# Seven-product projections of q, k and v, and the Fourier projection as a stage of its own

## The chip, the cores and the metric

The kernel runs on one core of a Trainium2 chip. The metric is the device time of one execution in microseconds. TensorE (PE) multiplies, VectorE (DVE), ScalarE (ACT) and GpSimd (POOL) work on tiles, SyncE (SP) issues DMAs, and DMA queues move data between HBM and the on-chip memory. Products accumulate in PSUM banks of 128 rows by 512 columns of fp32.

## The reference

One encoder block over 2048 tokens and 16 meta tokens put ahead of them, of width 1024:

```python
h += W_out [ RMSNorm_a(GQA attention group) ++ RMSNorm_f(Fourier group) ]  # from one W_in on RMSNorm(h)
h += W_down relu(W_up RMSNorm(h))^2
```

`W_in` has 1536 columns: 512 for q (4 heads of 128), 256 for k and 256 for v (2 heads each), and 512 for u. q and k are RMS-normed per head and rotated by an axial rope, and attention is softmax(q k^T / sqrt(128)) v over all 2064 tokens. u goes through `fft2(u, axes=(token, channel)).real` in four groups of 128 channels, and each group through a 128 by 128 matrix. Both groups are normed and go through `W_out`, the sum is the residual for a feed-forward layer of 4096 hidden units, and the 2048 real tokens leave through a last RMSNorm. All is fp32.

## The kernel before

**Arithmetic.** Each fp32 operand of a product is split in a high part (a cast on ACT, L70, or L73 with a scale per row) and a low part (source minus high on DVE, L71 or L74). `mm3` (L77) multiplies them with three matmuls, L80 to L82: high by high, high by low, low by high. `NG`=4 is the number of Fourier groups, `KT`=8 that of 128-row pieces of the width.

**Projections.** The tokens go in 8 pairs of 128. `prep(j)` (L274) norms a pair, transposes it on TensorE (L291) and splits it into `hth` and `htl`. `proj_qkv(j)` (L365) makes `pq` and `pkv` of both token tiles, each as 8 pieces by 3 matmuls of 512 columns. `proj_u(j)` (L331) makes u with the channels as rows: 4 groups by 8 pieces by 3 matmuls of 256 columns (272 in the last pair, which carries the meta tokens along). u stands in `UA`; from pair 4 on it is at once added to and subtracted from its mirror image, the sum in `EV`, the difference in `UA`. `post(j, a, ..)` (L389) works on a finished tile: squares on ACT (L408), the rest by DVE (L190, L414 to L422), transposes and splits, and stores to `q_d`, `k_d`, `v_d`, `v_n`. The weights are loaded (`wraw`) and split (`wh`, `wl`) at the start, row piece by row piece.

**Order of the work.** A generator per piece of side work is advanced between groups of matmuls (`side`), and a scheduler of the language then places each engine's instructions in the order it takes for best; the engines carry them out in that order. In the last pair, `proj_u` runs ahead of `proj_qkv`, and beside the latter run the folds (`fold`, `fold_even`, L506 to L517): each adds and subtracts halves of `EV` and `UA`, for the four groups, on DVE with a copy on ACT.

**Behind the projections.** `fourier()` (L658) makes four transforms: products `pa` with the channel matrices (L570), their splits `ahi` (ACT) and `alo` (DVE, L576), and products `py` with token tables (`thi`, `tlo`). `out_f` (L909) multiplies the result by its part of `W_out` (`pof`). Beside both runs attention, in steps counted from 0; each unit makes scores `s`, running maxima `M`, exponentials `S`, sums `acc` and products `o`. `mix(gen, n, a0, a1, skip)` advances a generator of n pieces and attention from step a0 to a1 together:

```python
    mix(with_weights(four, 9), 19, 0, FLEAD, SKIP - 1)
    mix(itertools.islice(of, 34 - HELD), 34 - HELD, FLEAD, need[0])
    mix(of, HELD, need[0], need[0] + LEAD)
```

`FLEAD` is 30 and `need[0]` is 84, so the transforms have 30 attention steps beside them and `out_f` 54. The later stages (attention's output product, `up`, `down`) are the same in both kernels; some of them use the scheme of seven products that the change brings to the projections.

## Time and profile before

| what | value |
|---|---|
| runs of the kernel | 2291.73, 2293.10, 2293.55 us (median 2293.1) |
| span of the profiled execution | 2291.4 us |
| TensorE busy | 2278.1 us, 99% |
| DVE busy | 1718.7 us, 75% |
| ACT busy | 1280.6 us, 56% |
| GpSimd busy | 184.0 us, 8% |
| granted TensorE clock | 0.9 or more of full speed in each of 40 slices |
| moved by DMA | 307.23 MB, mean 134 GB/s |

The profiled span is the time from the first to the last instruction of one execution; the runs are timed apart from it, and their median lies 1.7 us above the span. Busy time counts work alone, not the waits. In the windows, a row has a stretch of the span, then busy us and instruction count of each engine in it, the granted clock, the mean busy share of the DMA queues and their rate. In a timeline row stand the start, the length, the engine, the line, and the tiles (output, arrow, inputs).

### The profile page before, as it was taken

The numbers are of one execution on the slowest core, as the hardware profiler recorded it, in microseconds if no ns is written. First come the engines' busy times: TensorE is split into PE (matmuls) and PEld (weight loads), VectorE is DVE, ScalarE is ACT, GpSimd is POOL, SyncE is SP. The second block draws the span as 40 slices with busy tenths as digits, with TensorE's granted clock in tenths as the row PEclk, the third lists the DMA queues.
The fourth block names the chain that finished last, engine by engine and source line by source line (L and its number), as shares of the span: only waits on it lengthen the run. The fifth ranks groups of instructions, "written<-read, shape, count | busy, mean of one in ns | idle before, by whom it ended". The sixth has DMA issues, their size and how long they took to land.

```text
span 2291.4 us, 30005 instructions
## 1 busy us (share of the span) xinstructions
PE 2278.1 (99%) x10846; PEld 1883.0 (82%) x10846; DVE 1718.7 (75%) x2448; ACT 1280.6 (56%) x2303; POOL 184.0 (8%) x235
## 2 busy tenths in 40 slices
PE   9999999999999999999999999999999999999998
PEld 7888988777888888888888888888888888888887
DVE  6435588999986877986887877885875656697796
ACT  6443356566665655665765775664665545543344
POOL 2212120222000000000000100000000000200000
PEclk9999999999999999999999999999999999999999
DMA  6343252543533222333342453224454444865442
GB/s 213 100 119 102 78 169 79 190 137 120 166 117 108 96 87 79 114 114 106 97 157 87 157 175 104 92 82 170 140 177 158 152 152 156 303 193 165 129 138 83
DMA packets 178069, 307.23 MB, mean 134 GB/s; under 512 B 14960, under 2 KB 63728, under 8 KB 177536
## 3 DMA queue, kind: packets, MB, share of 16 engines
q1 hardware_dynamic: 159136, 262.89, 34.9%
q0 software_dynamic: 18640, 42.16, 6.2%
q8 instruction: 85, 1.39, 0.3%
q14 instruction: 64, 0.52, 0.1%
q10 hardware_dynamic: 144, 0.26, 0.0%
HBM read 225.27 MB, written 79.99 MB: 133 GB/s over the span
## 4 chain that ended last, share of the span: by engine, by line
PE 94%; DVE 3%; DMA 1%; ACT 1%; issue 1%; POOL 0%; SPq 0%; POOLq 0%; DVEq 0%; ACTq 0%
PE pdn L80 5%; PE pdn L82 5%; PE pdn L81 5%; PE pup L80 5%; PE pup L82 5%; PE pup L81 5%; PE s L80 3%; PE s L82 3%; PE s L81 3%; PE ux L80 2%; PE ux L81 2%; PE ux L82 2%; PE dx L80 2%; PE dx L82 2%; PE dx L81 2%; PE o L81 2%
## 5 line engine op out<-in xcount | busy, mean ns | idle before, releaser
L80 PE MATMUL pdn<-wh_dn,ah 128*128 128x512 f32 x512 | 201.5, 394 | 0.2 <-ACT r L1154 0.2
L80 PE MATMUL pup<-mTh,wh_up 128*128 128x512 f32 x512 | 201.5, 394 | 0.0
L81 PE MATMUL pup<-mTl,wh_up 128*128 128x512 f32 x512 | 200.7, 392 | 0.0
L82 PE MATMUL pup<-mTh,wl_up 128*128 128x512 f32 x512 | 200.4, 391 | 0.0
L81 PE MATMUL pdn<-wl_dn,ah 128*128 128x512 f32 x512 | 199.9, 390 | 0.0
L82 PE MATMUL pdn<-wh_dn,al 128*128 128x512 f32 x512 | 198.7, 391 | 0.0
L773 ACT COPY S<-s 128x512 f32<-128x512 f32 x256 | 148.4, 584 | 55.6 <-PE s L82 48.5
L70 ACT CAST wh_up<-wr_up 128x512 fp32r<-128x512 f32 x128 | 79.4, 620 | 164.3 <-PE pup L81 76.5
L832 DVE TENSOR_TENSOR S<-S,mb 128x1024 f32<-128x1024 f32 x128 | 154.8, 1218 | 8.4 <-ACT mb L803 8.2
L71 DVE TENSOR_TENSOR pl<-S,ph 128x512 fp32r<-128x512 f32 x196 | 132.3, 696 | 11.0 <-ACT ph L70 10.7
L833 ACT ACTIVATE S<-S 128x1024 f32<-128x1024 f32 x114 | 120.7, 1060 | 34.7 <-DVE S L832 34.1
L70 ACT CAST wh_dn<-wr_dn 128x512 fp32r<-128x512 f32 x128 | 79.1, 620 | 107.9 <-PE pdn L82 52.6
L71 DVE TENSOR_TENSOR wl_up<-wr_up,wh_up 128x512 fp32r<-128x512 f32 x128 | 87.6, 687 | 68.1 <-ACT wh_up L70 63.3
L839 DVE TENSOR_TENSOR acc<-acc,S 128x1024 f32<-128x1024 f32 x110 | 134.1, 1219 | 1.3 <-ACT S L833 1.1
L71 DVE TENSOR_TENSOR wl_dn<-wr_dn,wh_dn 128x512 fp32r<-128x512 f32 x128 | 87.2, 687 | 60.2 <-ACT wh_dn L70 51.8
L70 ACT CAST ph<-S 128x512 fp32r<-128x512 f32 x196 | 118.7, 620 | 15.9 <-PE o L82 12.5
L70 ACT CAST ah<-a 128x1024 fp32r<-128x1024 f32 x56 | 58.5, 1048 | 118.2 <-issue 60.8
L779 DVE TENSOR_TENSOR M<-M,S 128x1024 f32<-128x1024 f32 x96 | 118.0, 1229 | 6.7 <-ACT S L773 6.0
L80 PEld LDWEIGHTS pdn<-wh_dn,ah 128*128 128x128 f32 x512 | 96.1, 188 | 23.5 <-ACT r L1154 3.6
L80 PE MATMUL s<-q,kt 128*128 128x512 f32 (+1 forms) x272 | 113.0, 415 | 0.1
L82 PEld LDWEIGHTS pdn<-wh_dn,al 128*128 128x128 f32 x512 | 96.2, 188 | 19.9
L82 PEld LDWEIGHTS pup<-mTh,wl_up 128*128 128x128 f32 x512 | 96.2, 188 | 19.4
(345 smaller groups left out, 6413.0 us busy)
## 6 DMA issues: line engine op xcount, KB each, us to landing
wr_up<-in_w_up_dram SPq DMA_DIRECT2D x128, 256.0 KB, 2.8
wr_dn<-in_w_down_dram SPq DMA_DIRECT2D x128, 256.0 KB, 2.6
a<-s_d SPq DMA_DIRECT2D x42, 512.0 KB, 3.6
R<-in_w_up_dram SPq DMA_DIRECT2D x16, 1024.0 KB, 5.2
s_d<-s SPq DMA_DIRECT2D x64, 256.0 KB, 2.2
d<-in_w_down_dram SPq DMA_DIRECT2D x26, 512.0 KB, 5.0
s_d<-c SPq DMA_DIRECT2D x48, 256.0 KB, 2.4
x<-in_x_dram SPq DMA_DIRECT2D x16, 512.0 KB, 4.9
```

What stands on the lines that cost most here:

```text
L70: self.high = nc.scalar.copy(hi, src)
L71: self.low = nc.vector.tensor_tensor(lo, src, f32v(hi), op=ALU.subtract)
L80: nc.tensor.matmul(out, a[0], b[0], start=first, stop=False, skip_group_check=chain)
L81: nc.tensor.matmul(out, a[0], b[1], start=False, stop=False, skip_group_check=chain)
L82: nc.tensor.matmul(out, a[1], b[0], start=False, stop=last, skip_group_check=chain)
L773: nc.scalar.copy(S[:, i % 2], ps)
L779: nc.vector.tensor_tensor(M, M, S, op=ALU.max)
L832: nc.vector.tensor_tensor(S, S, mb, op=ALU.subtract)
L833: nc.scalar.activation(p, S, AF.Exp, scale=ISQ)
L839: nc.vector.tensor_tensor(acc, acc, p, op=ALU.add)
```

## The change

**Seven products.** For a token pair, the product of the 2 by 2 blocks (two token tiles by two halves of the width) with the 2 by 2 blocks of weights (two halves of the width by the columns of q and of k, v) is made from seven block products instead of eight. Each takes a form of the tokens (a block, or a sum or difference of blocks) and a form of the weights. `prep` makes the seven token forms from four groups of transposes; `form` splits each and stores it to HBM (`f_d`, 512 KB each). `w_forms` makes the forms of weights 3 to 7 at the start; forms 1 and 2 are plain blocks. `project` runs the products in the order 1, 2, 6, 5, 7, 3, 4, 84 matmuls of 512 columns per pair, and DVE adds partial results (`c`).

**u as a stage.** `proj_u` is gone. When the last pair is projected, the memory of the weight forms is released, and `u_forms` makes those of u over it. `u_stage` loads the stored token forms again (`hg`, 1 MB each, three buffers) and makes u for 1024 tokens at a time with products of 512 columns, 336 matmuls; `u_meta` adds 80 narrow matmuls for the meta tokens. Attention starts in this stage: 56 steps run beside it. The folds stand behind the stage, then the transforms with steps 56 to 64, and `out_f` with steps 64 to 84.

```diff
-FLEAD = 30
-SKIP = 5
+ULEAD = 56
+FLEAD = 64
+U_FIRST = 4
+HF_BUFS = 8
+W_BUFS = 16
+C_BUFS = 6
+HG_BUFS = 3
+ORDER = "1265734"
...
+    def form(j, name, src):
+        t = tp.tile([P, 2, 4, P], R32, name=f"hf{name}_{j}", tag="hf", bufs=HF_BUFS)
+        split(t[:, 0], t[:, 1], src.rearrange("p (k n) -> p k n", k=4))
+        nc.sync.dma_start(f_d[name, j // 4][:, :, j % 4], f32v(t.rearrange("p l k n -> p l (k n)")))
+        F[j, name] = t
...
+        ps = {}
+        for a in range(2):
+            for h in range(2):
+                yield
+                p = ps[a, h] = tbank(f"pt_{j}_{a}_{h}")
+                for i in range(4):
+                    k = 4 * h + i
+                    nc.tensor.transpose(p[:, i * P:(i + 1) * P], xs[j, a][:, k * P:(k + 1) * P], ident)
+                if a == 0:
+                    form(j, "12"[h], p)
+                elif h == 0:
+                    a21 = row(f"a21_{j}")
+                    nc.scalar.copy(a21, p)
+        s1, s2, s4 = (row(f"s{i}_{j}") for i in (1, 2, 4))
+        nc.vector.tensor_tensor(s1, ps[1, 1], a21, op=ALU.add)
+        nc.vector.tensor_tensor(s2, ps[0, 0], s1, op=ALU.subtract)
+        form(j, "6", s2)
+        form(j, "5", s1)
+        nc.vector.tensor_tensor(a21, a21, ps[0, 0], op=ALU.subtract)
+        form(j, "7", a21)
+        yield
+        nc.vector.tensor_tensor(s4, ps[0, 1], s2, op=ALU.add)
+        form(j, "3", s4)
+        form(j, "4", ps[1, 1])
...
+    def w_forms(k, raws, put):
+        b11, b12, b21, b22 = raws
+        g0, g1 = c_mix(k), c_mix(k + 4)
+        nc.gpsimd.tensor_tensor(b11, b12, b11, op=ALU.subtract)
+        nc.scalar.activation(b22, b22, AF.Copy, scale=g1)
+        split(*put("5"), b11, g0)
+        nc.vector.scalar_tensor_tensor(b11, b11, g0, b22, op0=ALU.mult, op1=ALU.subtract)
+        yield
+        split(*put("6"), b11)
+        yield
+        nc.vector.scalar_tensor_tensor(b12, b12, g0, b22, op0=ALU.mult, op1=ALU.subtract)
+        split(*put("7"), b12)
+        yield
+        split(*put("3"), b22)
+        yield
+        nc.vector.scalar_tensor_tensor(b21, b21, g1, b11, op0=ALU.mult, op1=ALU.add)
+        split(*put("4"), b21)
...
+    for k in range(KT):
+        load_w(k, 512)
+    for k in (4, 0, 5, 1, 6, 2, 7, 3):
         load_w(k, 0)
     drain(prep(0))
     load_x(1)
     for k in range(KT):
+        split(*W["12"[k // 4]][k % 4], raws[k, 512], c_mix(k))
+    drain(*[w_forms(k, [raws[i] for i in ((k, 512), (k, 0), (k + 4, 512), (k + 4, 0))],
+                    lambda n, k=k: W[n][k]) for k in range(4)])
+    ws.release()
...
+    def project(j, nxt):
+        X, Y, c = None, None, {}
+        for name in ORDER:
+            if name == "1":
+                X = bank(f"px_{j}")
+            elif name in "25":
+                Y = bank(f"py{name}_{j}")
+            o = Y if name in "253" else X
+            t = F.pop((j, name))
+            for k in range(4):
+                mm3(nc, o, (t[:, 0, k], t[:, 1, k]), W[name][k], name in "125" and k == 0, k == 3, True)
+            if name in "165":
+                c[name] = cp.tile([P, 512], F32, name=f"c{name}_{j}", tag="c", bufs=C_BUFS)
+                nc.scalar.copy(c[name], o)
+            elif name == "4":
+                pend.append(post(j, 1, c["5"], X))
+            else:
+                of = c[{"2": "1", "7": "5", "3": "6"}[name]]
+                nc.vector.tensor_tensor(of, of, o, op=ALU.add)
+                if name == "3":
+                    pend.append(post(j, 0, c["6"], c["1"]))
+            side(nxt)
...
+    for j in range(LAST + 1):
...
+        project(j, nxt)
+        drain(nxt)
+    spread_m()
+    pm = bank("pkv_m")
+    for k in range(KT):
+        t = MT_["m"][k // 4]
+        mm3(nc, pm[:MR], (t[:, 0, k % 4], t[:, 1, k % 4]), W["12"[k // 4]][k % 4], k == 0, k == KT - 1)
+    pend.append(post("m", 0, None, pm))
...
+    wq.release()
...
+    chan_dft()
...
+    def u_forms():
+        for k in range(4):
+            r = tp.tile([P, D], F32, name=f"wur_{k}", tag="x", bufs=3).rearrange("p (l n) -> p l n", l=2)
+            for i in range(2):
+                nc.sync.dma_start(r[:, i], w_in[(k + 4 * i) * P:(k + 4 * i + 1) * P, 1024:1536])
+            put = lambda n: (WU[n][:, 0, k], WU[n][:, 1, k])
+            b = [r[:, 0, :256], r[:, 0, 256:], r[:, 1, :256], r[:, 1, 256:]]
+            split(*put("1"), b[0], c_mix(k))
+            split(*put("2"), b[2], c_mix(k + 4))
+            drain(w_forms(k, b, put))
...
+    def u_stage():
+        for b in range(2):
+            X, Y = {}, {}
+            def place(t, G, s):
+                if b == 0:
+                    return t[:, G, META:META + 1024].rearrange("p (c s n) -> p c s n", s=2, n=P)[:, :, s]
+                return t[:, G, 1:1025].rearrange("p (c s n) -> p c s n", s=2, n=P)[:, :, 1 - s]
+            for name in ORDER:
+                h = []
+                for e in range(2):
+                    h.append(hg.tile([P, 4, 4, P], R32, name=f"hg{name}_{b}_{e}", tag="hg", bufs=HG_BUFS))
+                    nc.sync.dma_start(f32v(h[e].rearrange("p c k n -> p c (k n)")), f_d[name, b][:, e])
+                for g in range(2):
+                    if name == "1":
+                        X[g] = bank(f"ux_{b}_{g}")
+                    elif name in "25":
+                        Y[g] = bank(f"uy{name}_{b}_{g}")
+                out = lambda g: (Y if name in "253" else X)[g]
+                for e in range(2):
+                    for g in range(2):
+                        for k in range(4):
+                            for l in range(2 - e):
+                                nc.tensor.matmul(out(g).rearrange("p (c n) -> p c n", n=P),
+                                                 WU[name][:, l, k, g * P:(g + 1) * P], h[e][:, :, k],
+                                                 start=name in "125" and e + k + l == 0, stop=e == 1 and k == 3,
+                                                 skip_group_check=True)
+                        if e == 1:
+                            G, s = {"1": (g, 0), "6": (2 + g, 0), "5": (2 + g, 1), "4": (g, 1),
+                                    "2": (g, 0), "7": (2 + g, 1), "3": (2 + g, 0)}[name]
+                            y = out(g).rearrange("p (c n) -> p c n", n=P)
+                            d = place(UA, G, s)
+                            if b:
+                                y = y[:, ::-1, ::-1]
+                                v = place(EV, G, s)
+                                nc.vector.tensor_tensor(v, v if name in "273" else d, y, op=ALU.add)
+                                nc.vector.tensor_tensor(d, d, y, op=ALU.subtract)
+                            elif name in "273":
+                                nc.vector.tensor_tensor(d, d, y, op=ALU.add)
+                            else:
+                                nc.scalar.copy(d, y)
+                    yield
...
+    u_forms()
+    us = u_stage()
+    for _ in range(U_FIRST):
+        side()
+        next(us)
+    u_meta()
+    drain(*pend)
...
+    mix(us, 28 - U_FIRST, 0, ULEAD)
+    wu.release()
+    hg.release()
+    ft = Lines(tc.alloc_tile_pool(name="ft", bufs=1, reuse_waits="tile"), small)
+    for src in (EV, UA):
+        for g in range(NG):
+            fold(src, g)
+        for g in range(0, NG, 2):
+            fold_even(src, g)
+    load_tables(0)
+    fp = Lines(tc.alloc_tile_pool(name="fp", bufs=1, reuse_waits="tile"), small)
+    four = fourier()
...
-    mix(with_weights(four, 9), 19, 0, FLEAD, SKIP - 1)
+    mix(with_weights(four, 10), 20, ULEAD, FLEAD)
```

The next rows show DVE at the start, before: `wl1024` are lows of the weights of q, k and v, in the order of the row pieces, and `htl` lows of the first token pair.

```order
L74 SCALAR_TENSOR_TENSOR wl1024_0_213<-wraw0_0_141,cols_94,wh1024_0_212 128x512
L71 TENSOR_TENSOR htl_0_0_182<-pt_0_0_176,hth_0_0_181 128x512
L74 SCALAR_TENSOR_TENSOR wl1024_0_213<-wraw512_0_143,cols_94,wh1024_0_212 128x512
L71 TENSOR_TENSOR htl_0_1_191<-pt_0_1_185,hth_0_1_190 128x512
L74 SCALAR_TENSOR_TENSOR wl1024_1_219<-wraw0_1_145,cols_94,wh1024_1_218 128x512
L71 TENSOR_TENSOR htl_0_2_200<-pt_0_2_194,hth_0_2_199 128x512
L71 TENSOR_TENSOR htl_0_3_209<-pt_0_3_203,hth_0_3_208 128x512
L74 SCALAR_TENSOR_TENSOR wl1024_1_219<-wraw512_1_147,cols_94,wh1024_1_218 128x512
L74 SCALAR_TENSOR_TENSOR wl1024_2_225<-wraw0_2_149,cols_94,wh1024_2_224 128x512
```

After, at the same engine, the last rows ahead of the first addition of a partial result (`c1`): `wl4_0` to `wl4_3` are lows of the weight form 4, which the seventh product of the first pair reads, and L343 makes that form.

```order
L343 SCALAR_TENSOR_TENSOR wraw512_5_213<-wraw512_5_213,cols_83,wraw512_1_205 128x512
L343 SCALAR_TENSOR_TENSOR wraw512_6_215<-wraw512_6_215,cols_83,wraw512_2_207 128x512
L77 TENSOR_TENSOR wl4_0_193<-wraw512_4_211,wh4_0_192 128x512
L77 TENSOR_TENSOR wl4_1_195<-wraw512_5_213,wh4_1_194 128x512
L77 TENSOR_TENSOR wl4_2_197<-wraw512_6_215,wh4_2_196 128x512
L343 SCALAR_TENSOR_TENSOR wraw512_7_217<-wraw512_7_217,cols_83,wraw512_3_209 128x512
L232 TENSOR_TENSOR sm_1_0_417<-ss_1_0_412 128x1
L232 TENSOR_TENSOR sm_1_1_429<-ss_1_1_424 128x1
L191 TENSOR_SCALAR ms_x_419<-sm_1_0_417 128x1
L191 TENSOR_SCALAR ms_x_431<-sm_1_1_429 128x1
L77 TENSOR_TENSOR wl4_3_199<-wraw512_7_217,wh4_3_198 128x512
L481 TENSOR_TENSOR c1_0_410<-c1_0_410,py2_0_436 128x512
```

The weights' lows came one by one with the products that read them; now there are sums of blocks ahead of them, and the last low stands behind all other forms.

DVE at the folds, before: the last folds of `UA`, the copies of the remainder and the splits of tables stand ahead of the normalization of the pair's tiles (`qn`), which waits for the products of q and of k, v.

```order
L516 TENSOR_TENSOR folde2_3114<-UA_69 128x514
L536 COPY rem0_3122<-EV_70 128x4x2
L536 COPY rem0_3122<-EV_70 128x4x3
L517 TENSOR_TENSOR UA_69<-UA_69 128x2x257
L536 COPY rem0_3122<-EV_70 128x4x2
L536 COPY rem0_3122<-EV_70 128x4x3
L536 COPY rem0_3122<-EV_70 128x4x2
L536 COPY rem0_3122<-EV_70 128x4x3
L551 TENSOR_TENSOR tlo0_1_3140<-traw0_1_3136,thi0_1_3138 128x2x258
L554 TENSOR_TENSOR thi0_4_3144<-traw0_4_3142,thi0_4_3144 32x2x258
L190 TENSOR_SCALAR ms_h0_3236<-sq_14_3227 128x6
L414 TENSOR_TENSOR qn_14_3228<-pq_7_0_3147,rs_h0_3238 128x512
```

After, the folds stand behind the additions of the last u product (`ux_1`) and behind attention's operations (`S`, `M`, `acc`, `pl`).

```order
L577 TENSOR_TENSOR EV_2598<-UA_2597,ux_1_1_3451 128x4x128
L873 TENSOR_TENSOR S_2_10_3647<-S_2_10_3647,mb_2_3762 128x1024
L578 TENSOR_TENSOR UA_2597<-UA_2597,ux_1_1_3451 128x4x128
L820 TENSOR_TENSOR M_3_3917<-M_3_3917,S_3_8_4027 128x1024
L880 TENSOR_TENSOR acc_2_3809<-acc_2_3809,S_2_10_3647 128x1024
L77 TENSOR_TENSOR pl_2_11_0_4031<-S_2_10_3647,ph_2_11_0_4030 128x512
L77 TENSOR_TENSOR pl_2_11_1_4038<-S_2_10_3647,ph_2_11_1_4037 128x512
L873 TENSOR_TENSOR S_2_12_3676<-S_2_12_3676,mb_2_3762 128x1024
L608 TENSOR_TENSOR fold0_4063<-EV_2598 128x516
L608 TENSOR_TENSOR fold1_4067<-EV_2598 128x516
L609 TENSOR_TENSOR EV_2598<-EV_2598 128x516 x2
```

What was placed before the end of the projections is now placed after the end of the u stage.

TensorE at that place, after: the last of attention's products (`o`, `s`) behind the u stage, and then the first products of the transform (`pa0`), which read the folded `EV`.

```order
L87 MATMUL o_2_3810<-pl_2_11_1_4038,vt_0_1_2_3482 128x512
L88 MATMUL o_2_3810<-ph_2_11_1_4037,vt_0_1_2_3482 128x512
L86 MATMUL s_3_12_4289<-q_3_3825,kt_0_1_3_3476 128x512
L87 MATMUL s_3_12_4289<-q_3_3825,kt_0_1_3_3476 128x512
L88 MATMUL s_3_12_4289<-q_3_3825,kt_0_1_3_3476 128x512
L86 MATMUL s_3_13_4419<-q_3_3825,kt_0_1_3_3476 128x512
L87 MATMUL s_3_13_4419<-q_3_3825,kt_0_1_3_3476 128x512
L88 MATMUL s_3_13_4419<-q_3_3825,kt_0_1_3_3476 128x512
L86 MATMUL o_2_3810<-ph_2_13_0_4227,vt_0_1_3_3484 128x512
L672 MATMUL pa0_0_4142<-cw0_2602,EV_2598 128x128 x2
L672 MATMUL pa0_1_4151<-cw0_2602,EV_2598 128x128 x2
```

Between the last matmul of u and the first of the transform stand 31 of attention, of which these are the last nine; before, the transform followed products of q, k and v.

314 lines of the change are left out of this document (97 added, 217 removed).

## The prediction

> **What bounds the kernel now.** I read first the page's head with the busy times, then its chain of waits.
>
> ```profile
> span 2291.4 us, 30005 instructions
> PE 2278.1 (99%) x10846; PEld 1883.0 (82%) x10846; DVE 1718.7 (75%) x2448; ACT 1280.6 (56%) x2303; POOL 184.0 (8%) x235
> PE 94%; DVE 3%; DMA 1%; ACT 1%; issue 1%; POOL 0%; SPq 0%; POOLq 0%; DVEq 0%; ACTq 0%
> ```
>
> TensorE is busy 99% of the span, and 94% of the chain that ends last is matmuls. Whoever takes matmuls away gains their issue time, and whoever opens a hole on TensorE pays for it in full. So I need two things: the price of a matmul, and how full the other engines are where the change puts work. The windows by stage give the second (columns: window, length, busy us of PE, weight loads, DVE, ACT and POOL, granted TensorE clock, DMA share, GB/s).
>
> ```profile
> 0.00:20.00 20.00, 17.61 (x67) 11.90 (x68) 12.57 (x26) 13.44 (x26) 2.11 (x7) 1.00 0.89 315
> 11.30:45.00 33.70, 33.70 (x199) 29.91 (x198) 25.87 (x47) 25.38 (x66) 8.67 (x8) 1.00 0.63 212
> 45.00:309.90 264.90, 264.24 (x1580) 232.89 (x1579) 134.03 (x303) 107.16 (x349) 49.89 (x55) 1.00 0.34 99
> 100.00:133.30 33.30, 33.30 (x206) 29.83 (x206) 14.32 (x31) 13.55 (x43) 5.96 (x8) 1.00 0.40 111
> 133.30:166.60 33.30, 33.30 (x208) 29.88 (x207) 16.16 (x38) 14.66 (x48) 7.16 (x8) 1.00 0.38 111
> 273.60:295.60 22.00, 22.00 (x126) 19.28 (x126) 20.06 (x47) 10.39 (x27) 0.00 (x0) 1.00 0.04 13
> 309.90:424.50 114.60, 113.80 (x699) 94.20 (x697) 103.33 (x162) 73.74 (x136) 17.12 (x23) 1.00 0.49 140
> 424.50:584.90 160.40, 158.90 (x712) 124.55 (x711) 153.80 (x218) 97.54 (x186) 40.69 (x52) 1.00 0.48 157
> ```
>
> From 11.3 to 309.9 the projections run on a TensorE without holes; DVE is half idle there. The Fourier transforms (to 424.5) and their output product (to 584.9) follow, with attention mixed in, DVE at 90% and 96%. After 584.9 nothing changes.
>
> The price of a matmul is the distance of two starts in the timeline, since the records overlap.
>
> ```profile
> 177.61 0.39 PE L81 MATMUL pkv<-wl,hth 128*128 128x512 f32 x1
> 177.84 0.40 PE L82 MATMUL pkv<-wh,htl 128*128 128x512 f32 x1
> 183.15 0.28 PE L81 MATMUL pu<-htl,wh 128*128 128x256 f32 x1
> 183.27 0.28 PE L82 MATMUL pu<-hth,wl 128*128 128x256 f32 x1
> 424.35 0.28 PE L934 MATMUL pys<-ones,ysq 128*128 128x1 f32 x2
> 424.49 0.47 PE L80 MATMUL pof<-wfh,yh 128*128 128x512 f32 x1
> ```
>
> 512 columns cost 0.228 us (0.23 here), 256 cost 0.120, and a very narrow one about 0.07 (two records in 0.14 us).
>
> **The change part by part: what goes.** q, k and v of a token pair go from 96 to 84 matmuls of 512 columns: 8 × 12 × 0.228 = 21.9 us gone. The u projection loses 672 matmuls of 256 columns and 96 of 272 (0.128, scaled from 256) and gets 336 of 512: 80.6 + 12.3 − 76.6 = 16.3 us gone. The 16 meta tokens need 80 narrow ones, 5.6 us. TensorE saves 32.6 us. Everything below is holes.
>
> **Start: +11.4.** The rows are the chain's first matmuls, the first u product, and DVE's cadence for a split with a scale and for a plain subtraction.
>
> ```profile
> 9.34 1.97 PE pt L291 x16
> 11.31 0.24 PE pq L80
> 33.03 0.28 PE L80 MATMUL pu<-hth,wh 128*128 128x256 f32 x1
> 10.55 0.75 DVE L74 SCALAR_TENSOR_TENSOR wl<-wraw,cols,wh 128x512 fp32r<-128x512 f32 x1 [1.10 <-ACT wh L73]
> 14.94 3.40 DVE L74 SCALAR_TENSOR_TENSOR wl<-wraw,cols,wh 128x512 fp32r<-128x512 f32 x5
> 287.12 0.70 DVE L517 TENSOR_TENSOR EV<-EV 128x516 f32<-128x516 f32 x1
> 287.73 0.69 DVE L507 TENSOR_TENSOR UA<-UA 128x516 f32<-128x516 f32 x1
> ```
>
> Before, 96 matmuls ran from 11.3 to 33.0 (0.226 each) with DVE just keeping ahead. After, the seventh product of the first pair needs the last form of the weights, and DVE has by then 24 scaled operations (3.40 / 5, so about 0.66 apart when back to back) and 27 plain ones (0.605 apart): 15.9 + 16.3 = 32.2 us from 10.5, to 42.7. TensorE ends that pair near 43.3; unstalled it would be 11.3 + 84 × 0.228 + 1.4 for transposes = 31.9. The hole is 11.4 us. Lower end 10 (some subtractions overlap the loads), upper 15 (DVE's 1.10 us wait for ACT, as in the row of 10.55, at three of the forms).
>
> **DMA beside the projections: +8.4.** Each pair now stores seven forms of 512 KB, 3.67 MB. At the start 315 GB/s went with a share of 0.89, so 354 at a share of one, and 3.67 MB is 10.4 us. A pair before took 33.3 us, as long as the two windows of 100.0 and 133.3, and 0.39 (the mean of their 0.40 and 0.38) of the queues' time: 13 us. That is 23.4 us per pair, against 84 × 0.228 + 3 (transposes, as now) = 22.2 on TensorE. TensorE has to wait for form buffers, which are freed by stores: 1.2 × 7 pairs = 8.4. At the highest share seen, 0.89, a pair is 26.3 and the loss 28.7; if queues overlap better the loss is 0. I take 8.4, the nearest row's rate. DVE (16.2 now, about 19 after) and ACT stay below 22.2. [...]
>
> **End of the projections: +5.** The weight forms of u lie in the memory of the q, k, v forms, so they are made after the last product, by DVE, behind the normalization of the last token tile.
>
> ```profile
> 33.49 0.38 DVE L190 TENSOR_SCALAR ms_h<-sq 128x6 f32<-128x6 f32 x1 [0.25 <-ACT t L408]
> 39.18 0.42 DVE L422 TENSOR_TENSOR qn<-t,t 128x256 f32<-128x256 f32 x1
> 46.02 0.42 DVE L71 TENSOR_TENSOR vt<-vr,vt 128x256 fp32r<-128x256 f32 x1
> 46.36 0.42 DVE L420 TENSOR_TENSOR t<-qn,cg 128x256 f32<-128x256 f32 x1
> ```
>
> That normalization is 6.1 us, some 1.5 us of squares ahead of it; the lows that the first product needs of the fourth weight row come 29 operations of 256 columns later (0.34 apart): 7.6 + 9.9 = 17.5 us after the last product. TensorE has the 24 meta matmuls (5.5), the DFT's two products and transposes (3) and 18 u matmuls (4.1) before it needs them: 12.6. Hole 5; 3 if the operations mesh better, 12 if DVE stays behind up to the third product.
>
> **Start of u: +5.** Two 1 MB loads feed each 24 matmuls (5.5 us).
>
> ```profile
> R<-in_w_up_dram SPq DMA_DIRECT2D x16, 1024.0 KB, 5.2
> ```
>
> At 354 GB/s the pair needs 5.9 us, so the first products run at the loads' pace until attention comes in, and the loads of q, k and v join. Between 0 (loaded before the last product ends) and 10.4 (two latencies in the open) I take the middle.
>
> **Folds: +14.** Before, the 24 folds of u ran beside the last q, k, v products: the window of 273.6 to 295.6 shows DVE at 20.06 and TensorE at 22.00 of 22.00. That cover is gone: they now follow the last u product, and the transform follows them.
>
> ```profile
> 273.62 0.69 DVE L506 TENSOR_TENSOR fold<-EV 128x516 f32<-128x516 f32 x1
> 293.94 0.69 DVE L517 TENSOR_TENSOR UA<-UA 128x514 f32<-128x514 f32 x1
> 354.32 1.22 DVE L832 TENSOR_TENSOR S<-S,mb 128x1024 f32<-128x1024 f32 x1
> 355.45 1.22 DVE L776 TENSOR_TENSOR M<-S,S 128x1024 f32<-128x1024 f32 x1
> 309.89 3.74 PE L570 MATMUL pa<-cw,EV 128*128 128x128 f32 x32
> 361.63 2.48 DVE L576 TENSOR_TENSOR alo<-pa,ahi 128x512 fp32r<-128x512 f32 x4
> ```
>
> After the last u product DVE has two adds of it, four 1024-wide attention operations (1.13 from start to start) and two of 512: 4 × 1.13 + 4 × 0.605 = 6.9 us, 7.1 with their gaps. Then 12 operations up to the last fold of EV, 7.3: the first transform product can start 14.5 us after it, and TensorE has 31 attention matmuls (7.1) in between: hole 7.7. The products of EV take 3.7, to 18.7; the last fold of UA and the six remainder copies end near 23, hole 4.3; the low halves (0.6 each) another 2. Together 14. At the least DVE's queue makes 11.6; with ACT waits inside the attention operations 20. [...]
>
> **Fourier: +5.** The transforms now have 8 attention steps beside them instead of 30. Each of four waits for its low halves: 2.5 us in the open at worst (the row of four), so 10; 0 if the 8 steps stand in the right places.
>
> The sum is −32.6 + 11.4 + 8.4 + 5 + 5 + 14 + 5 = +16.2: span 2307.6. The runs of before have the median 2293.1, 1.7 above the profiled span, so 2309.3.
>
> **The rivals.** *The holes are covered* (faster): the loads and stores keep up, and attention matmuls stand where the u weights, the start of u and the transforms wait. Then only the start (11.4) and DVE's sure part of the folds (11.6) are paid: −32.6 + 23.0 = −9.6, 2283.5. For it: DVE is half idle in the projections and DMA is at 0.38. It decides when the four smaller terms fall below 9.6 in all. *No change* (within 0.2%, about 4.6 us, what a measurement of this kernel can tell from none): two of the four are hidden, so −9.6 + 10 = 0.4, 2293.5. *The stores bound the projections*: at share 0.89 the loss is 28.7, not 8.4: 2329.6. For it: the projections' transfers already take 13 us for 3.7 MB, 292 GB/s at a share of one. *That the change doesn't remove the matmuls* is all but excluded: the order of the program counts 672 of 512 for q, k, v and 336 for u. [...]
>
> **Chances.** Forecast 0.48 (own range 2299 to 2325, the ends of start, weights, folds and Fourier taken half together), stores as bound 0.17, no change 0.14, faster 0.21. Slower is 0.48 + 0.17 = 0.65. The range leaves out about a tenth on each side: 2281 (beyond it the covered case with a fold hole of nine) to 2334 (stores as bound with the clock estimate's few us).
>
> **What would show it.** Right: the first pair's products end near 43 with TensorE waiting for DVE on the weights' lows; a hole of some 8 us and one of 4 at the folds with DVE as releaser; DMA share near 0.9 in the projections and short waits for form tiles; the projections' pair at 23 to 24 us. Wrong: pairs at 22.2 with a DMA share of 0.8 or less (the DMA term), holes below 3 us at the folds, or a DVE stall anywhere in the u stage, which I cost at nothing: its operations there, at the durations of the rows above, come to an estimated 118 us beside 190 us of matmuls.

## The result, and the profile after

The changed kernel takes 2369.2 us (median of 4 runs, 2368.2 to 2372.4) against 2292.8 us for the kernel before (4 runs, 2291.7 to 2293.6): a ratio of 1.0335, interval 1.032 to 1.035. It is slower by 76.4 us. The sum forecast +16.2, and a range that ended at 2334. One of the timed runs below, of the bare start of u, took 5257.9 us and is left out.

The head of the profile after, and its chain:

```profile
span 2366.5 us, 29548 instructions
PE 2285.8 (97%) x10398; PEld 1858.5 (79%) x10398; DVE 1802.5 (76%) x2599; ACT 1327.7 (56%) x2390; POOL 196.5 (8%) x243
PE 84%; DVE 6%; ACT 2%; issue 1%; POOL 1%; DMA 1%; SPq 0%; POOLq 0%; ACTq 0%; DVEq 0%
```

The 448 fewer matmuls are there (10846 to 10398). But TensorE is idle for 2366.5 − 2285.8 = 80.7 us, where it was 13.3, and its share of the chain fell from 94% to 84%; 6% of the chain is DVE now. The windows say where (columns as in the prediction):

```profile
11.30:45.00 33.70, 12.49 (x38) 7.76 (x36) 33.34 (x53) 23.87 (x45) 6.91 (x6) 0.72 0.61 222
35.00:40.00 5.00, 0.00 (x0) 0.00 (x0) 5.00 (x9) 2.93 (x9) 0.00 (x0) 0.50 0.09 26
135.00:165.00 30.00, 27.32 (x136) 21.82 (x136) 24.78 (x49) 21.36 (x70) 7.46 (x9) 1.00 0.92 297
254.40:286.80 32.40, 21.12 (x64) 13.85 (x62) 26.00 (x64) 17.43 (x48) 9.81 (x10) 0.74 0.76 236
290.00:295.00 5.00, 5.00 (x34) 5.00 (x34) 0.50 (x4) 0.35 (x2) 1.31 (x2) 0.70 1.08 415
295.00:300.00 5.00, 5.00 (x23) 5.00 (x24) 0.24 (x2) 0.17 (x1) 4.03 (x8) 0.50 1.17 383
299.70:440.00 140.30, 140.22 (x564) 100.62 (x565) 103.25 (x131) 65.94 (x102) 8.29 (x12) 0.99 0.67 219
440.00:480.00 40.00, 28.70 (x121) 23.69 (x120) 39.46 (x63) 23.47 (x40) 0.00 (x0) 0.79 0.11 32
440.00:542.40 102.40, 88.84 (x590) 81.05 (x589) 91.12 (x166) 57.12 (x108) 0.71 (x1) 0.92 0.22 64
659.80:2366.50 1706.70, 1698.20 (x7640) 1396.44 (x7639) 1297.62 (x1712) 972.09 (x1558) 66.67 (x91) 1.00 0.41 134
```

Four places: the first pair (TensorE works 12.5 of 33.7 us), the projections (27.3 of 30), the start of u (21.1 of 32.4) and the folds (28.7 of 40). In the rows of the first pair, the start of u and the folds the granted clock is below 1.00 (0.72, 0.74 and 0.79). From 299.7 to 440, the rest of the u stage, TensorE has no holes. The last row is the part behind `out_f`, which was 1706.5 us before (2291.4 − 584.9): the whole loss lies ahead of it. What TensorE waits for there, in the list of waits to 700 us (tile, line, releaser, line: us in all, times, longest):

```profile
PE pt L283 <- ACT x L234: 20.8, 8, 16.9
PE ptq L400 <- DVE qn L376: 15.9, 12, 3.1
PE py L86 <- ACT wh L79: 4.9, 2, 4.4
PE pa L672 <- DVE alo L678: 4.5, 2, 3.2
PE pa L672 <- DVE EV L619: 3.9, 1, 3.9
PE ux L565 <- DVE wu L80: 3.6, 2, 3.2
PE uy L565 <- DMA hg<-f_d: 2.7, 1, 2.7
```

The 4.4 us for a cast `wh` lie at 15 to 19.5, inside the first pair. And TensorE's timeline at the marks used below:

```profile
28.91 0.40 PE L88 MATMUL py<-wh,hf 128*128 128x512 f32 x1
46.24 1.11 PE L283 MATMUL pt<-ident,x 128*128 128x128 f32 x4 [16.94 <-ACT x L234]
60.48 0.39 PE L88 MATMUL px<-wh,hf 128*128 128x512 f32 x1
60.71 0.39 PE L86 MATMUL px<-wh,hf 128*128 128x512 f32 x1
215.94 1.40 PE L283 MATMUL pt<-ident,x 128*128 128x128 f32 x8 [1.82 <-ACT jk L229]
218.82 2.12 PE L283 MATMUL pt<-ident,x 128*128 128x128 f32 x8 [1.48 <-ACT jk_m L229]
254.04 0.39 PE L88 MATMUL pkv_m<-wh,hm 128*96 128x512 f32 x1
287.12 0.26 PE L535 MATMUL pum<-hm,wu 128*128 128x16 f32 x1
287.24 0.26 PE L533 MATMUL pum<-hm,wu 128*128 128x32 f32 x1
297.17 0.36 PE L535 MATMUL pum<-hm,wu 128*128 128x16 f32 x1
297.39 0.37 PE L533 MATMUL pum<-hm,wu 128*128 128x32 f32 x1
464.62 6.21 PE L672 MATMUL pa<-cw,EV 128*128 128x128 f32 x32 [3.88 <-DVE EV L619]
474.05 1.17 PE L672 MATMUL pa<-cw,rem 128*96 128x128 f32 x4 [3.22 <-DVE alo L678]
```

With them the loss over the sum, 2366.5 − 2307.6 = 58.9, is placed. The first pair's products end at 60.9 (the row of 60.48 is its 84th matmul, that of 60.71 the first of the next pair) where 43.3 was forecast: 17.6. The projections end at 254.4, where the forecast's terms give 309.9 − 21.9 − 92.9 (all of u's matmuls) + 11.4 + 8.4 = 214.9: 39.5, and less the 17.6, 21.9 for pairs 1 to 7. From there to 659.8 it is 405.4, forecast 584.9 + 16.2 − 214.9 = 386.2: 19.2.

Counted by 84 matmuls each and named from 0 (the first pair is pair 0), pairs 1 to 5 take 27.1, 26.5, 25.8, 25.1 and 26.4 us, pair 6 takes 21.2 and pair 7 34.0. Against the forecast 23.4 that is 13.9 too much for pairs 1 to 5 and 8.3 for the last two. The last two belong together: the transposes of pair 7's tokens run behind pair 6's products (end 212.9) instead of among them, and wait there for the squares of their own normalization on ACT (the rows of 215.94 and 218.82); the granted clock is 0.50 from 220 to 225 us.

### The profile page after: what moved, and what is told of

Same layout as the page of the kernel before. It is cut to its first block, busy times and chain, and to the rows that moved or that the text cites. A ratio compares the mean times of both kernels' runs of the same rounds, so it can differ in the third digit from the quotient of the medians.

```text
span 2366.5 us, 29548 instructions
## 1 busy us (share of the span) xinstructions
PE 2285.8 (97%) x10398; PEld 1858.5 (79%) x10398; DVE 1802.5 (76%) x2599; ACT 1327.7 (56%) x2390; POOL 196.5 (8%) x243
## 4 chain that ended last, share of the span: by engine, by line
PE 84%; DVE 6%; ACT 2%; issue 1%; POOL 1%; DMA 1%; SPq 0%; POOLq 0%; ACTq 0%; DVEq 0%
PE pdn L86 5%; PE pdn L88 5%; PE pdn L87 5%; PE pup L86 5%; PE pup L87 5%; PE pup L88 5%; PE s L86 2%; PE ux L86 2%; PE ux L88 2%; PE ux L87 2%; PE dx L87 2%; PE dx L86 2%; PE s L88 2%; PE s L87 2%; PE dx L88 2%; PE o L86 2%
```

## Experiments

Each time stands beside the changed kernel's 2369.2; intervals are those of the ratio to the kernel before, whose median lay between 2292.7 and 2293.1 in all of these comparisons. The edits are shown in their main lines. The first four experiments take the suspects that the lists above name: the normalization of pair 1's tokens (16.9 us), the transfers and the head norms beside the pairs, and the meta products.

**Normalize pair 1 early.**

```diff
+    first = prep(1)
+    next(first)
     drain(*[w_forms(k, ...) for k in range(4)])
...
-        nxt = prep(j + 1) if j < LAST else iter(())
+        nxt = first if j == 0 else prep(j + 1) if j < LAST else iter(())
```

> Edit: the norm of token pair 1 is issued ahead of the weight forms 3 to 7. In the changed kernel TensorE stands from 29.3 to 46.2 us with the transposes of pair 1 at its head, which wait for a norm that stands on DVE behind all weight lows, and 36 ready or nearly ready matmuls of pair 0 (products 6 and 7, then 3) are queued behind them. Theory 'in-order wait': these products run as their lows come, and products of pair 1 fill in; pair 0 ends 12 us earlier or more (60.9 now), and the time falls by 12 to 20 us. Rival 'the weights themselves': products 6, 7 and 4 wait for DVE's lows anyway (the last at 45.5), the hole only changes its name, and the time falls by less than 5 us.

2362.8 us (1.0301, 1.0286 to 1.0317): 6.5 less. The products now end at 56.3, and TensorE still stands idle for 10.4 us from 29.27, so neither expectation was met in full: the normalization was the last releaser, not the only thing late.

**No stores of six of the seven forms.**

```diff
-        nc.sync.dma_start(f_d[name, j // 4][:, :, j % 4], f32v(t.rearrange("p l k n -> p l (k n)")))
+        if name == "1":
+            nc.sync.dma_start(f_d[name, j // 4][:, :, j % 4], f32v(t.rearrange("p l k n -> p l (k n)")))
...
-                    nc.sync.dma_start(f32v(h[e].rearrange("p c k n -> p c (k n)")), f_d[name, b][:, e])
+                    nc.sync.dma_start(f32v(h[e].rearrange("p c k n -> p c (k n)")), f_d["1", b][:, e])
```

> Edit: only form 1 of the tokens is stored; the u stage loads form 1 for all seven products (same loads, u is then not the reference's). 48 of 56 stores of 512 KB are gone from the projections. Theory 'DMA' (the prediction's term): pairs 1 to 6 fall from 26.3 us each to about 22.5 and the time by 20 to 29 us. Rival 'latency between engines': the pairs stay within 0.7 us of 26.3, since TensorE waits there for DVE and ACT and not for a DMA; the time changes by less than 6 us.

2359.4 us (1.029, 1.0272 to 1.0307): 9.8 less. The pairs 1 to 5 still take 27.1, 26.2, 25.6, 25.6 and 24.7 us, and the wait for `qn` between 60 and 250 us stays (11.5 us in the changed kernel):

```profile
PE ptq L401 <- DVE qn L377: 13.0, 13, 1.3
```

Pairs 1 to 5 come to 129.3 us instead of 130.9; 6.8 of the 9.8 us lie in the last two (48.3 instead of 55.1), where pair 7's transposes now stand among pair 6's products. In the changed kernel no wait of TensorE from 60 to 250 us is put down to a DMA. So the stores are not why a pair takes 26 us, and that 9.8 lies near the 8.4 of the prediction is chance: the cost is in another place than that term. Why the order of the last two pairs changes with the stores is open.

**No pow in the head norms.**

```diff
-        rs = rstd_of(tp, ss[:rows, h0:], 6 - h0, HD, f"h{h0}", rows)
+        rs = mhalf
```

> Edit: the normalization of q and k uses a constant in place of the reciprocal root from GpSimd (squares stay on ACT; q and k are then not the reference's). That takes about 3 us out of the chain from a tile's last product to its transposes, and nearly no work from any engine. Theory 'latency between engines': the holes ahead of the transposes of q (1.2 us, two per pair) close, pairs 1 to 6 take some 24 us, and the time falls by 12 to 20 us. Rival 'DMA': nothing changes by more than 4 us. Rival 'DVE's load': the pairs stay at 26, since DVE's work is the same.

2350.4 us (1.0251, 1.0235 to 1.0266): 18.8 less. Pairs 2 to 6 take 22.6 to 24.3 us, and the wait for `qn` between 60 and 250 us falls from 11.5 us to

```profile
PE ptq L400 <- DVE qn L376: 3.0, 3, 1.3
```

Pairs 1 to 5 gain 10.0 us, most of their 13.9; the last two gain 9.6, again with pair 7's transposes ahead of pair 6's end. So the chain of latencies makes most of the loss in pairs 1 to 5, and the power is one link of it: squares on ACT, mean on DVE, the power on GpSimd, four DVE operations on q, transposes on TensorE. In one tile of the changed kernel, on DVE and then on TensorE:

```profile
97.42 0.17 DVE L191 TENSOR_SCALAR ms_h<-sq 128x6 f32<-128x6 f32 x1 [0.72 <-ACT t L362]
99.03 0.69 DVE L368 TENSOR_TENSOR qn<-c,rs_h 128x512 f32<-128x512 f32 x1 [1.44 <-POOL rs_h L193]
101.52 0.69 DVE L376 TENSOR_TENSOR qn<-t,t 128x512 f32<-128x512 f32 x1
```

```profile
102.26 0.66 PE L400 MATMUL ptq<-ident,qn 128*128 128x128 f32 x4 [1.22 <-DVE qn L376]
```

From the mean to the transposes it is 4.8 us, and TensorE runs out of other work 1.22 us too early. In the kernel before, the waits of DVE from 45 to 273 us show the GpSimd link at the same length (16.5 / 12 = 1.4 us)

```profile
DVE qn L414 <- POOL rs_h L192: 16.5, 12, 1.4
```

and TensorE's own waits in that stretch were one, for something else:

```profile
PE pt L291 <- ACT x L250: 0.7, 1, 0.7
```

The link was always there. What stood in front of it was u: 96 independent matmuls of 256 columns, 96 × 0.120 = 11.5 us per pair, and these are what the change moved away. No run puts them back; that their absence opens the holes is read from the two traces, and the run with late transposes below supports it.

**No meta products.**

```diff
-    u_meta()
+    for t in (UA, EV):
+        nc.gpsimd.memset(t[:, :, 0:META] if t is UA else t[:, :, 0:1], 0.0)
```

> Edit: the 80 narrow matmuls of the meta tokens' u are left out (their u is zero). The profile gives them 286.8 to 299.6 us, 12.8 us, where 5.6 was forecast, with the weight loads busy all the time and the clock down to 0.5. Theory 'they cost what they take': the time falls by 11 to 16 us (more than 12.8 if the clock comes back earlier). Rival 'they cover a wait': the loads of token forms for the next product come in behind them, and the time falls by less than 5 us.

2362.5 us (1.0304, 1.0289 to 1.032): 6.7 less of the 12.8 that those products occupy. The rest came back as a wait that the changed kernel did not have, for a load of token forms:

```profile
298.20 2.08 PE L565 MATMUL ux<-hg,wu 128*128 128x512 f32 x4 [5.32 <-DMA hg<-f_d]
```

**Start: pair 1's transposes behind product 3.** On top of the early normalization. `done[0]` is the last matmul of the product before; the lines that record it are left out here and in the next diff.

```diff
+                with tc.issue_after(done[0]) if j == 1 else nullcontext():
...
-            side(nxt)
+            side(iter(()) if j == 0 and name in "12657" else nxt)
```

> Edit: as in the run with the early norm, and the transposes of pair 1 are also put behind product 3 of pair 0 in TensorE's order, ahead of product 4. With the early norm alone TensorE still stood 10.4 us at those transposes (29.3 to 39.6) with products 6, 7 and 3 queued behind them, while DVE worked without a gap from 20 to 46 us. Theory 'in-order wait': TensorE now does products 6, 7 and 3 between 33 and 42 us, pair 0's last matmul ends near 49 (61 in the changed kernel, 56 with the early norm), and the time falls by 10 to 15 us against the changed kernel. Rival 'DVE is the bound anyway': what pair 1 needs from DVE (its seven forms) comes as late as before, pair 1 starts late instead, and the gain stays at the 6.5 us of the early norm, within 2.

2373.0 us (1.0348, 1.0331 to 1.0366): 3.8 more than the changed kernel, hardly beyond what runs differ by, and 10.2 more than with the early normalization alone. The hole did not move; its releaser did. First TensorE, then ACT in this run's timeline:

```profile
46.01 0.79 PE L86 MATMUL px<-wh,hf 128*128 128x512 f32 x1 [16.69 <-ACT c L481]
```

```profile
44.85 0.62 ACT L76 CAST wh<-wraw 128x512 fp32r<-128x512 f32 x1 [0.65 <-DVE wraw L345]
45.38 0.58 ACT L481 COPY c<-px 128x512 f32<-128x512 f32 x1
```

Product 6 adds to product 1's bank and so waits for the copy of that bank, which ACT makes behind the cast of the very last weight form. Both expectations failed, and the run named the next suspect: the tile `c` is allocated from a pool that lies over the raw weights' memory, free only when the last form has been read.

**Transposes of q later in the pair.**

```diff
+        late = not m and j < LAST
+        for _ in range((5 if a else 3) if late else 0):
+            yield
...
-            for h in range(4):
-                nc.tensor.transpose(ps[:, h * P:(h + 1) * P], qn[:, h, :], ident)
+            with tc.issue_after(done[0]) if late else nullcontext():
+                for h in range(4):
+                    nc.tensor.transpose(ps[:, h * P:(h + 1) * P], qn[:, h, :], ident)
```

> Edit: the transposes of the normalized q of pairs 0 to 6 are put later in TensorE's order, behind product 6 (first token tile) and product 3 (second) of the next pair; no work is taken away. The constant in place of the reciprocal root took pairs from 26.1 to 24.1 us and the time down by 18.8 us. Theory 'latency between engines': TensorE no longer meets transposes whose normalization is still under way, pairs 1 to 6 take 24 to 24.7 us, and the time falls by 9 to 17 us. Rival 'the next wait takes its place': the later stores, buffers or the norm of the next pair hold TensorE instead, pairs stay within 0.7 us of 26.1, and the time changes by less than 4 us.

2360.3 us (1.0294, 1.0279 to 1.031): 8.9 less, with nothing left out of the computation. Pairs 2 to 5 take 24.9 us each, and the last two 48.2 instead of 55.1. Two waits are left in a pair such as these:

```profile
129.01 0.66 PE L284 MATMUL pt<-ident,x 128*128 128x128 f32 x4 [1.28 <-DVE qt L77]
147.65 0.66 PE L284 MATMUL pt<-ident,x 128*128 128x128 f32 x4 [0.86 <-ACT x L234]
```

**Matmuls into the low-clock stretch of the folds** (nine extra products whose result is overwritten).

```diff
+            for _ in range({0: 5, 4: 4}.get(nt, 0) if tr == 0 else 0):
+                nc.tensor.matmul(ps, EV[:, 0, QUART + 2:QUART + 2 + P], cw[0], start=True, stop=True)
```

> Edit: work is added. Five matmuls of 512 columns in plain fp32 (about 0.85 us each) are put in the hole ahead of the first product of the transform and four in the one ahead of the fifth; their results are overwritten. They read a folded part of EV, so they run inside the holes (3.9 and 3.2 us in the changed kernel). Theory 'clock': between 455 and 480 us the granted clock, 0.5 to 0.8 in the changed kernel, comes back to 0.9 or more from 465 on, the products after the holes run at full speed, and the time falls by 2 to 6 us though work was added. Rival 'the clock there is of no account, only DVE is waited for': the time stays within 1 us or rises by up to 3.

2369.8 us (1.0335, 1.032 to 1.0351): no difference. The first hole is filled and the granted clock is 1.00 from 465 to 470 us (0.55 in the changed kernel), but the next wait grew, and the four matmuls (eight records) meant for the second hole waited themselves and ran behind it, after 5.00 us without a matmul at a granted clock of 0.69 (470 to 475):

```profile
475.35 5.35 PE L671 MATMUL pa<-cw,EV 128*128 128x512 f32 x8 [5.55 <-DVE alo L680]
```

So the second half of the edit did not do what it was made for, and the run does not show what the clock alone costs at the folds.

**Half of the folds ahead of the last u product**, with temporaries of their own; those of `UA` for the other two groups between the transform's first products.

```diff
+                    if b and name == "3" and e == 1:
+                        for t in (EV, UA):
+                            fold(t, 2)
+                            fold(t, 3)
+                            fold_even(t, 2)
...
```

> Edit: the folds of groups 2 and 3, whose u is complete after the sixth of the seven products, are put ahead of the last product of the u stage, and the folds of UA for groups 0 and 1 behind the first transform, which doesn't read them. Same work. Theory 'folds without cover': the holes of 3.9 and 3.2 us ahead of the transform shrink to under 2 in all, the clock there stays up, and the time falls by 6 to 12 us. Rival 'attention's DVE work is the bound there': the folds displace exponentials and sums, TensorE waits for those inside the u stage instead, and the time falls by less than 3 us.

2371.6 us (1.0344, 1.0329 to 1.0359): 2.4 more, within what runs differ by. The transform's waits on DVE shrank to one of 2.1 us and one of 0.3; attention's took their place, in the list of waits from 420 to 560 us:

```profile
PE o L87 <- DVE pl L77: 6.5, 5, 2.5
PE o L86 <- ACT ph L76: 4.3, 2, 3.3
```

In the changed kernel these two are 2.4 and 1.8 there. DVE has that much to do in this stretch (39.46 of 40 us in the row of 440 to 480), in whatever order.

**Partial results in memory of their own** for the first pair.

```diff
-                c[name] = cp.tile([P, 512], F32, name=f"c{name}_{j}", tag="c", bufs=C_BUFS)
+                if j == 0:
+                    c[name] = tp.tile([P, 512], F32, name=f"c{name}_{j}", tag="c0", bufs=3)
+                else:
+                    c[name] = cp.tile([P, 512], F32, name=f"c{name}_{j}", tag="c", bufs=C_BUFS)
```

> Edit: the three partial results (c) of pair 0 get memory of their own; in the changed kernel they lie over the raw weights, whose memory is released first. With the transposes put late TensorE stood just as long (29.3 to 46.0 us), then at product 6, waiting for ACT's copy of product 1's result: product 6 adds into that bank, so it can't start before the copy, and the copy can't start before DVE's last form has read the raw weights beneath. In ACT's order the copy moves from behind the last weight cast to behind that of form 3. Theory 'memory reuse': the hole from 29.3 to 46.2 falls to some 6 us, pair 0 ends near 49, the time falls by 10 to 14 us. Rival 'the weights' lows': products 6, 7 and 4 wait for DVE as before, the time falls by less than 5.

2355.4 us (1.0278, 1.026 to 1.0295): 13.9 less from the address of three tiles. The first pair ends at 53.0 instead of 60.9, and the later pairs, whose order changes too, bring a further 4.1 by the end of the projections (242.4 instead of 254.4). ACT's first copy of `c`, in the changed kernel and then in this one:

```profile
46.10 0.57 ACT L476 COPY c<-px 128x512 f32<-128x512 f32 x1
```

```profile
28.20 0.58 ACT L479 COPY c<-px 128x512 f32<-128x512 f32 x1
```

It moves in ACT's order from behind the last cast of a weight form into the middle of them.

The biggest hole left is one that the forecast had in it, DVE at the weights' last forms (until 45.5), here with sums of `c` behind them:

```profile
46.34 0.76 PE L86 MATMUL px<-wh,hf 128*128 128x512 f32 x1 [5.55 <-DVE c L484]
```

**The same with the early normalization.** The diff is the two above together.

> Edit: the same, and the early norm of pair 1. Theory 'memory reuse': the early norm adds only what it brought in products of pair 1 that fill holes, 2 to 6 us beyond the run with own memory alone, so 13 to 18 us under the changed kernel. Rival 'the weights' lows': no more than the 6.5 us of the early norm alone.

2353.6 us (1.0262, 1.0247 to 1.0277): 15.7 less; the first pair ends at 48.5. On top of the own memory the early normalization brings 1.8, within what runs differ by, though the first pair ends 4.5 us earlier.

**Few weight forms for u** (five of the seven forms of u's weights not made).

```diff
+    for n, o in zip("67534", "11122"):
+        WU[n] = WU[o]
...
-            drain(w_forms(k, b, put))
```

> Edit: of the u weights only forms 1 and 2 are made and used for all seven products (u is then not the reference's): 16 operations on DVE in place of 40 or so after the last product of q, k, v. Theory 'forms in the open' (the prediction's term of 5 us): the waits of 0.4 and 3.2 us for the weights close and the clock is kept, 4 to 9 us less. Rival 'the loads are next': TensorE waits for the token forms' loads instead, less than 3 us.

2372.1 us (1.0342, 1.0326 to 1.0357): no gain. The waits for `wu` shrank from 3.6 us to one of 1.4; this one came, where 2.7 stood:

```profile
278.47 8.08 PE L567 MATMUL uy<-hg,wu 128*128 128x512 f32 x24 [4.85 <-DMA hg<-f_d]
```

**Meta products made twice.**

```diff
+            terms = terms + terms
```

> Edit: work is added: the narrow matmuls of the meta tokens are done twice (160 instead of 80; u of the meta tokens is then doubled). In the changed kernel they stand 0.111 us apart at first and 0.213 us from 292 us on, where the granted clock is 0.5 although TensorE has no gap. Theory 'narrow matmuls bring the clock down': nearly all of the added 80 run at 0.21, and the time rises by 14 to 19 us. Rival 'the low clock comes from the waits before them': the added ones run at 0.11 once the clock is back, and the time rises by 6 to 10 us.

2384.5 us (1.04, 1.0385 to 1.0416): 15.3 more for 80 narrow matmuls, 0.19 us each. TensorE has no gap in the whole stretch (5.00 of each 5.00 us), from 310 to 320 no DMA moves anything (0 GB/s), and the granted clock is still 0.50:

```profile
305.00:310.00 5.00, 5.00 (x26) 5.00 (x25) 0.33 (x2) 0.17 (x1) 0.00 (x0) 0.50 0.33 90
310.00:315.00 5.00, 5.00 (x25) 5.00 (x25) 0.00 (x0) 0.00 (x0) 0.00 (x0) 0.50 0.00 0
320.00:325.00 5.00, 5.00 (x19) 3.76 (x18) 0.00 (x0) 1.17 (x2) 0.00 (x0) 0.81 0.20 48
```

In the last row the 512-column products are on again, and the granted clock is 0.81.

**The three cures together**: own memory, early normalization, late transposes; all of the computation is done.

> Edit: three edits that each helped, together: own memory for the partial results of pair 0, the early norm of pair 1, and q's transposes put later in TensorE's order. All work of the changed kernel is done. Theory 'separate waits': the gains add, 15.7 + 8.9 = 24.6, so 2344.6 us (2341 to 2348). Rival 'one wait in several places': DVE's and ACT's chains are then behind elsewhere, and the gain stays at 16 to 20 us. By either it is still 2% or more over the kernel before.

2346.3 us (1.0233, 1.0218 to 1.0249): 22.9 less, of 15.7 + 8.9 = 24.6 from the parts; the projections end at 232.0 instead of 254.4. It is the best complete version, and 2.3% above the kernel before.

**A bare start of u**: no meta products, few weight forms, and one set of token forms loaded per half instead of seven.

```diff
+    for n, o in zip("67534", "11122"):
+        WU[n] = WU[o]
...
-            drain(w_forms(k, b, put))
...
-                h = []
-                for e in range(2):
+                if name == "1":
+                    h = []
+                for e in range(2 if name == "1" else 0):
...
-    u_meta()
+    for t in (UA, EV):
+        nc.gpsimd.memset(t[:, :, 0:META] if t is UA else t[:, :, 0:1], 0.0)
```

> Edit: at the start of the u stage three things are left out together: the u weight forms 3 to 7 (1 and 2 are used in their place), the narrow matmuls of the meta tokens, and the loads of token forms other than form 1 (it is used for all products; u is then not the reference's). Left out alone, the weight forms brought nothing (a wait of 4.9 us for loads took their place) and the meta tokens 6.7 of the 12.8 us they took (a wait of 5.3 us for a load took the rest). Theory 'each covers the other': with all three gone the time falls by 18 to 25 us (12.8 of meta tokens, 3.6 and 2.7 of waits, and the matmuls at half clock). Rival 'something else is next': normalization of the last tiles or attention's loads hold TensorE there, and the time falls by less than 12 us.

2342.0 us (median of three runs, 2341.5 to 2343.7; 1.0216, 1.0199 to 1.0233): 27.2 less, where the forms alone gave nothing and the meta products 6.7. Each covers the others. In the stretch where the changed kernel was busy for 21.1 of 32.4 us at a clock of 0.74, this one has:

```profile
254.40:286.50 32.10, 27.69 (x114) 20.59 (x113) 16.73 (x35) 14.63 (x34) 11.33 (x16) 0.95 0.97 295
```

The longest wait left there is 3.1 us for `qn`, the normalization of the last tokens.

**Eight attention steps moved from u to the transforms.**

```diff
-ULEAD = 56
+ULEAD = 48
```

> Edit: one size. 48 attention steps run beside the u stage and 16 beside the transforms, in place of 56 and 8. The prediction put 5 us on the transforms' having only 8 steps as cover. Theory 'cover': the waits in the transforms (1.2, 0.5, 0.5 us) and part of the holes at the folds close, the time falls by 3 to 7 us. Rival 'DVE is the bound there': it has 39.5 of 40 us of work from 440 to 480 us and attention steps bring it more work than they bring TensorE, so moving them behind the folds changes the time by less than 2 us or makes it longer.

2367.4 us (1.0322, 1.0305 to 1.0339): 1.8 less, no difference. More matmuls beside the transforms gain nothing, and the waits at the folds stay, 4.3 us for `EV` and 3.1 for `alo`.

**No folds.**

```diff
-    for src in (EV, UA):
-        for g in range(NG):
-            fold(src, g)
-        for g in range(0, NG, 2):
-            fold_even(src, g)
```

> Edit: the 24 folds are left out (the transforms then read unfolded u). Theory 'folds in the open' as the prediction had it: the holes of 3.9 and 3.2 us and the low clock behind them go, the time falls by 8 to 13 us. Rival 'DVE is the bound there': all of the folds' 15 to 16 us on DVE count, since DVE has no gap from 440 to 480 us, and the time falls by 14 to 20 us.

2358.0 us (1.0285, 1.0269 to 1.03): 11.2 less. That is what the folds in the open cost, DVE's work for them included.

## Why the prediction was wrong, point by point

The direction was right, the size was not: +16.2 forecast, +76.4 measured. Three steps failed, mostly because TensorE waits where the forecast let it work on: the first pair (17.6 us over), the pairs behind it (21.9), and the start of u with its narrow products (some 15).

**What goes (−32.6).** The products of 512 columns go at the forecast price (60.48 to 60.71 is 0.23). Wrong is the meta part, "5.6 us": it rests on a row of 1-column matmuls in a stretch with a granted clock of 1.00. The narrow ones of u stand 0.12 us apart (287.12 to 287.24) where 1.00 is granted (286.8 to 290.0) and 0.22 (297.17 to 297.39) where 0.50 is (295 to 300): 12.8 us in all, from 286.8 to 299.6, 7.2 more than forecast.

**Start (+11.4).** The step that failed is "the seventh product of the first pair needs the last form of the weights", read as: the other six do not. TensorE ran dry at 29.3, with three products done (1, 2 and 5, 36 matmuls). Product 6 waited for the copy `c`, `c` for memory in which the raw weights stood until the last form was made, and the next pair's transposes for a normalization that stood late on ACT. The DVE count itself was near: its last weight low was forecast for 42.7, and ends at 45.5.

```profile
44.81 0.69 DVE L77 TENSOR_TENSOR wl<-wraw,wh 128x512 fp32r<-128x512 f32 x1 [0.35 <-ACT wh L76]
```

But behind it stood 48 matmuls (10.9 us at 0.228 each; the granted clock is 0.53 from 45.5 to 50.0 and 0.86 from 45.5 to 60.9, and transposes of the next pair stand among them) instead of the last few, and the pair ended 17.6 us later than forecast. With own memory and the early normalization it ends at 48.5 instead of 60.9, and the kernel is 15.7 us faster.

**DMA beside the projections (+8.4).** "TensorE has to wait for form buffers" failed: none of TensorE's waits from 60 to 250 us is put down to a DMA, and without six of seven stores pairs 1 to 5 are only 1.6 us shorter in all. The queues do run near the forecast 0.9 (0.92 in the row of 135 to 165, 0.81 from 60.9 to 213.0), so that part of the sign was there without its effect. What stands in the term's place lies in "22.2 on TensorE", which has no waits in it, and in my check against it, which compared busy times of DVE and ACT. DVE's is as forecast (114.7 us from 60.9 to 213.0, 19.1 for each of six pairs), but I had not asked how long the chain from a tile's last product to its transposes is and what stands beside it: without u's matmuls between them, the transposes wait for the chain of ACT, DVE and GpSimd. Pairs 1 to 5 take 25.1 to 27.1 us, and with the power taken out of the chain 10.0 us less in all. The last two, 8.3 over, lose it with pair 7's transposes behind pair 6: in the runs without stores, without the power and with late transposes, where they stand ahead of its end, these two take 6.8 to 9.6 us less. The rival "stores bound the projections" had the size of a pair (26.3) by luck and not the cause; its 292 GB/s is 111 / 0.38 from the row of 133.3 to 166.6.

**End of the projections and start of u (+5 +5).** Too low. From 254.4 to 286.8 TensorE is idle for 32.4 − 21.1 = 11.3 us, and at a granted clock of 0.74 the 21.1 busy ones lose an estimated 0.26 × 21.1 = 5.5: 16.8 in place of 10. With the 7.2 of the meta products, an estimated 1.4 of lower clock behind them (granted 0.50 from 299.6 to 302.0 and 0.95 to 305.0: 0.50 × 2.4 + 0.05 × 3.0) and 1.7 at the folds (below), that places 17.1 of the 19.2. The causes that the prediction named, weight forms and loads, are there (3.6 and 3.5 us of waits), with the last tokens' normalization ahead of their transposes (3.8), which it had counted in DVE's queue alone; but they don't add up as terms: weight forms alone gain nothing, meta alone 6.7, all with the loads 27.2, which is 14.4 beside the 12.8 of the meta products.

**Folds (+14) and Fourier (+5).** Here the mechanism held: waits of 3.9 and 3.2 us with DVE as releaser, smaller than the 8 and 4 forecast. The sum came near partly by luck: from 440 to 542.4 TensorE is idle for 13.6 us, attention's waits included, and at 0.92 its 88.8 busy ones lose an estimated 7.1 to the clock, which the sum had left out; 20.7 together, for 19. The folds alone are worth 11.2 of it, as the run without them shows. Two figures of the working slipped: 14.5 − 7.1 is 7.4, and 14.5 + 3.7 is 18.2; with both the term is 14.2. The upper end of the range, 2334, holds a few us for the clock at these two holes, a term that no run shows: measured is a granted clock of 0.79 from 440 to 480, and the run with extra matmuls there, at 2369.8 us, doesn't separate what it costs. The 5 us for the lost cover of the transforms were not found: eight more steps of attention as cover gained 1.8, within what runs differ by. The sign "a DVE stall anywhere in the u stage" did not come up in its main part, where TensorE is busy for 140.22 of 140.30 us.

**What stays open:** what a pair loses beyond its 22.2 us when the transposes stand late (24.9; two waits of 1.28 and 0.86 are shown, the rest is not), why pair 7's transposes stand late in some versions and not in others, and how much of the loss at the folds is the lower clock (0.79 from 440 to 480). The seven products for q, k and v with the old u projection between them, the version that this study points to, was not tried.

## What to carry to other kernels

Work that is moved away is also a cover that is removed: before it is moved, list the waits that run beside it, each with the length of its chain from engine to engine, not only the busy time per engine. A tile that lies over released memory can wait for the last reader of what lay there, as the copies of `c` did (the first at 46.10 us, 28.20 in memory of its own); a tile on the critical path needs an address that nobody else is slow to free. When a run comes near a forecast number, look whether the time lies where the forecast put it. Where single edits exchange one wait for another, remove all suspects at once to see what the place is worth, and only then decide which to mend.

## What the runs showed of the hardware

A granted clock of 0.50 was measured with TensorE idle and with TensorE busy. In the changed kernel it stands in 35 to 40 us, where TensorE does nothing (0.00 of 5.00 us), and also in 295 to 300, where TensorE is busy for 5.00 of 5.00 us, up to 299.5 with matmuls of 16 and 32 columns and as many weight loads (the row counts 23 and 24). In the run with the meta products twice it stands in 305 to 315, in rows of 26 and 25 such matmuls with 25 weight loads each and TensorE busy for 5.00 of each 5.00 us. Whether the few columns or the weight load for each matmul go with the lower clock is not separated, and no run shows what sets it.

The transfers reached 415 GB/s in the row of 290 to 295, at a share of 1.08. That is 384 at a share of one (415 / 1.08), and the row of 135 to 165 makes 323 (297 / 0.92); the prediction took 354 from the start (315 / 0.89) for the stores. The rate at a share of one was not the same from stretch to stretch.
